# Score products in a row, program order on TensorE in both attentions, and a rotation made by transfers

## The chip, the cores and the metric

One core of a Trainium2 chip runs the whole program. The metric is device time in microseconds (us) of one execution; a measurement gives the median of several. The engines are TensorE (PE; its weight loads are listed apart as PEld), VectorE (DVE), ScalarE (ACT), GpSimd (POOL) and SyncE (SP), which issues the DMAs.

## The reference, cut to what matters

Sequence 512, width 1024, float32, two decoder stacks of two layers each. Two of the four mixers are attentions with pairs of maps:

```
# differential attention: 8 heads, two maps of width 64 each, shared k and v
s = einsum(q, k) * 64**-0.5 ; causal mask ; p = softmax(s)
a = p[map 0] - lam * p[map 1] ;  o = a @ v ;  o = rms_norm(o, g) * (1 - lambda_init) ;  out = o @ w_out
# sparse attention: 16 heads in 4 groups, rotary on the first 16 of 64 dims
q = rmsnorm(q) ; q_rope = partial_rope(q)
s_s = q_rope @ k_sel ; s_w = q_rope @ k_win          # both causal over 512 keys here: all 8 blocks are selected
out = gate_c * o_c + gate_s * softmax(s_s) @ v_sel + gate_w * softmax(s_w) @ v_win
```

`partial_rope` replaces dims (d, d+8), d < 8, by (x1 cos - x2 sin, x2 cos + x1 sin).

## The kernel before, in words

All activations lie transposed, in arenas of 128 x 512 slots: `arena_r` (fp32r, operands of products) and `arena_f` (fp32), and eight PSUM banks. Dense products split both factors into a high and a low part and make three products (L253 to L255, 128 x 512 each). Weights are streamed from HBM in chunks by SP (L92) and split by ACT (L106) and DVE (L107).

Both attentions run through `attend` (L797). Its units are (head, query tile t) in the differential attention and (tile pair T, query tile t, half hh) in the sparse one. In step s it makes the scores of unit s (`score`, L759) and their softmax, combines unit s-1 on DVE, multiplies unit s-3 with V (`value`, L970 and L1564) and calls `finish`, then `each` puts in other work, and last it transposes the maps of unit s-2 (L828) and copies them from PSUM (L832 on DVE, L834 on ACT). The other work are generators in `fill_q`: dense products of the next head's queries or of the output, a few products at each step.

`score` makes for each of the two maps the product with the high part of k, the product with the low part (L772), and a bf16 product of the identity with the causal mask, 128 columns wide (L777). For t below 2 both maps lie in one bank.

After a head's last query tile, `finish` of the differential attention copies the output from PSUM on ACT (L991), squares it on ACT (L993) and sums the columns on TensorE (L289). After heads 3 and 7 a root and a reciprocal follow on ACT and DVE (last L1003), and TensorE spreads the result over the columns (L312). A head's queries leave their dense product through DVE (L903), ACT (L906, twice) and DVE (L907, twice).

In the sparse attention `chain` (L1276) normalises and rotates one 128-row tile, one stage at each step while the tile before it is in `attend`: square, column sums (L1284) with a power on POOL (L1291) and a copy on ACT (L1293), transposes (L1297) and a scaling on DVE (L1299), the permutation as an fp32 product (L1303) with the multiplication by the sines (L1305), then `qout`: the rotated queries and a small attention over compressed keys (L1451, L1475).

In which order an engine works is mostly decided when the program is built: a list scheduler places every instruction as early as its own estimate of times allows, so an instruction of a later step can stand ahead of one that waits. Inside `in_order()` (L370) TensorE keeps the order in which the Python code issues its instructions; the other engines stay free. Before, that is used in `tail` (L326) and `group_halves` (L425) alone, not in `attend`.

Of the kernel before, what the change touches and what calls it, by code (L numbers as in the profile page):

```python
# [211 lines left out]
class Build:  # L212
    def __init__(self, nc, tc, ctx, src, vat):
        self.nc, self.tc, self.src, self.vat = nc, tc, src, vat
        pool = ctx.enter_context(tc.tile_pool(name="sb", bufs=1))
        psum = ctx.enter_context(tc.tile_pool(name="ps", bufs=1, space=bass.MemoryType.PSUM))
        self.pool = pool

        def sb(name, shape, dt=F32):
            return pool.tile(shape, dt, name=name, tag=name)  # L220

        self.sb = sb
        self.fill_q = deque()
        ra = sb("arena_r", [128, N_R, S], F32R)
        fa = sb("arena_f", [128, N_F, S])
        self.R = Arena([ra[:, i] for i in range(N_R)])
        self.F = Arena([fa[:, i] for i in range(N_F)])
        self.fa = fa
        self.P = Arena([psum.tile([128, S], F32, name=f"bank{i}", tag=f"bank{i}") for i in range(8)])
        self.W = Stream(nc, tc, pool, src["w"], src["w"].shape[0])  # L230
        self.vec = sb("vec", list(src["vec"].shape))
        self.cst = sb("cst", list(src["cst"].shape))
        self.small = sb("small", [128, 112])
        self.keep = sb("keep", [128, 16])
        self.sm_n = 0
        self.x = self.F.take(KD)
        self.xd = nc.dram_tensor("x_wait", (KD, 128, S), F32, kind="Internal").ap()
# [218 lines left out]
    def mm(self, out, a, b, start):  # L456
        self.nc.tensor.matmul(out, a, b, start=start, stop=False, skip_group_check=True)  # L457
# [298 lines left out]
        yield  # L756


    def score(self, q2, k2, t):  # L759

        n = 128 * (t + 1)
        banks = self.P.take(1 if t < 2 else 2)
        outs = []
        for c in range(2):
            if t < 2:
                o = banks[0].a[:, c * 256:c * 256 + n]
            else:
                o = banks[c].a[:, :n]
            first = c == 0 or t >= 2
            if isinstance(k2[c], (tuple, list)):  # L770
                for i, k in enumerate(k2[c]):
                    self.nc.tensor.matmul(o, q2[c][:, t * 128:(t + 1) * 128], k[:, :n], start=first and i == 0, stop=False,  # L772
                                          skip_group_check=True)
            else:
                self.nc.tensor.matmul(o, q2[c][:, t * 128:(t + 1) * 128], k2[c][:, :n], start=first, stop=False,
                                      skip_group_check=True)
            self.nc.tensor.matmul(o[:, n - 128:], self.ident_b, self.causal_b, start=False, stop=True,  # L777
                                  skip_group_check=True)
            outs.append(o)
        return banks, outs  # L780

    def softmax(self, banks, outs):
# [14 lines left out]
    def attend(self, units, score, combine, value, finish, fill=1, lag=1, share=True, each=None):  # L797

        nc = self.nc
        st = [None] * len(units)  # L800

        def comb(i):
            if 0 <= i < len(units):
                st[i] = combine(units[i], *st[i])

        for s in range(len(units) + lag + 1):
            if s < len(units):
                banks, outs = score(units[s])
                st[s] = self.softmax(banks, outs)
            comb(s - 1)  # L810
            i = s - lag - 1
            if 0 <= i < len(units):
                value(units[i], st[i])
                finish(units[i])
                st[i] = None
            if each is not None:
                each(s)
            else:
                self.fill(fill)
            i = s - lag  # L820
            if 0 <= i < len(units):
                t = units[i][1]
                n = 128 * (t + 1)
                res = []
                for c, m in enumerate(st[i]):
                    b = self.P.get()
                    for kt in range(t + 1):
                        nc.tensor.transpose(b.a[:, kt * 128:(kt + 1) * 128], m.a[:, kt * 128:(kt + 1) * 128], self.ident)  # L828
                    m.free()
                    d = self.F.get()  # L830
                    if share and (i + c) % 2 == 0:
                        nc.vector.tensor_copy(d.a[:, :n], b.a[:, :n])  # L832
                    else:
                        nc.scalar.activation(d.a[:, :n], b.a[:, :n], AF.Copy)  # L834
                    b.free()
                    res.append(d)
                st[i] = res


    def diff(self, update):  # L840
# [47 lines left out]
        khi, qs = {}, {}  # L888
# [48 lines left out]
        def score(u):  # L937
            h, t = u
            if t == dt[0] and h > 0:
                self.fill_all(qg[h])  # L940
                if h == 4:
                    self.fill_all(vg[3])
                    free([s for p in pk.xs for s in p])
                elif h == 2:
                    self.fill_all(vg[2])
            if t == dt[0] and h < 7:
                self.fill_q.append(qg[h + 1])
                if h < 2:
                    self.fill_q.append(vg[h + 2])
            if t == dt[2] and h < 7:  # L950
                kpack(h + 1)
            return self.score([q.a for q in qs[h]], [[khi[h][c].a, klo[h % 2][c].a] for c in range(2)], t)

        def combine(u, ps, sm):
            n = 128 * (u[1] + 1)
# [269 lines left out]
    def nsa(self, update):  # L1225
# [4 lines left out]
        V = [F.run(2) for _ in range(2)]  # L1230
        va = [self.fa[:, v[0].i:v[0].i + 2].rearrange("p a n -> p (a n)") for v in V]
        vb = [v.rearrange("p (t c) -> p t c", t=4) for v in va]
        kpad = [[R.take(2) for _ in range(4)] for _ in range(2)]
        for c in range(2):
            for g in range(4):
                lo = 64 * (1 - g % 2)
                nc.gpsimd.memset(kpad[c][g][1].a[lo:lo + 64].bitcast(F32), 0.0)
        C, Sn, misc = self.table(6), self.table(7), self.table(8)
        perm, bones = misc.a[:, 0:128], misc.a[:, 128:130]
        w2 = misc.a[:, 256:512]  # L1240
# [32 lines left out]
        nc.vector.tensor_tensor(rs2, rs, rs, op=ALU.mult)  # L1273
        nc.vector.tensor_scalar(rs2, rs2, 1.0 / 64, None, op0=ALU.mult)

        def chain(t, g, scale, out):  # L1276


            sq = F.get()
# [18 lines left out]
            sq.free()  # L1298
            nc.vector.scalar_tensor_tensor(t.a, t.a, self.v(g), b.a, op0=ALU.mult, op1=ALU.mult)  # L1299
            b.free()  # L1300
            yield
            b = P.get()
            nc.tensor.matmul(b.a, perm, t.a, start=True, stop=True)  # L1303
            rot = F.get()
            nc.vector.tensor_tensor(rot.a, b.a, Sn.a, op=ALU.mult)  # L1305
            b.free()
            yield from out(t, rot)
            t.free()
            rot.free()

        def split(src, m, both, hi, lo):

            r, o = slice(64 * m, 64 * m + 64), slice(64 - 64 * m, 128 - 64 * m)
            nc.scalar.activation(hi[r], src[r], AF.Copy)
            if both:
                nc.scalar.activation(hi[o], src[r], AF.Copy)
                nc.vector.tensor_tensor(lo[r], src[r], hi[r], op=ALU.subtract)
            else:
                nc.vector.tensor_tensor(lo[o], src[r], hi[r], op=ALU.subtract)

        def kout(c, i):
            def f(t, rot):
                nc.vector.tensor_tensor(t.a, t.a, C.a, op=ALU.mult)
                nc.vector.tensor_tensor(t.a, t.a, rot.a, op=ALU.add)
                for m in range(2):
                    split(t.a, m, True, kpad[c][2 * i + m][0].a, kpad[c][2 * i + m][1].a)
                yield
            return f

# [78 lines left out]
        raw = {}  # L1408
# [89 lines left out]
        def ahead(T):  # L1498
            while ("q", T) not in raw or side:
                self.fill(1)  # L1500
            ready.append((T, chain(raw.pop(("q", T)), "q_g", 0.125, qout(T))))

        def advance(n=1):
            while n and ready:
# [21 lines left out]
        def score(u):  # L1526
            T, t, hh = u
            g = 2 * (T // 4) + hh
            if (hh, t) == (0, to[0]):
                while ready and ready[0][0] <= T:  # L1530
                    advance()
                qp[T] = R.take(2)
                for m in range(2):
                    split(qr[T].a, m, False, qp[T][m].a, qp[T][m].a)
                qr[T].free()
            return self.score([qp[T][hh].a] * 2, [[s.a for s in kpad[c][g]] for c in range(2)], t)

        def combine(u, ps, sm):
            T, t, hh = u
# [149 lines left out]
def tables():  # L1689
# [14 lines left out]
    for o in (0, 8, 64, 72):  # L1704
        t[6, o:o + 8], t[7, o:o + 8] = np.cos(ang), np.sin(ang)
    for o in (0, 64):
        for d in range(8):
            t[8, o + d + 8, o + d] = -1.0
# [56 lines left out]
```

## Time and profile before

| | us |
|---|---|
| runs | 2692.94, 2693.13, 2695.53 |
| median | 2693.13 |
| the profiled execution | 2693.81 |
| its span, first to last instruction | 2692.0 |

Busy time of each engine in that span: PE 2657.0 us, DVE 1677.4, ACT 1197.9, POOL 117.9. A row of the timeline gives the start, the duration, the engine, the line, the operation with its tiles and shapes, how many are merged, and in brackets the idle time of the engine ahead of it with what ended it. Durations of products overlap, because they are pipelined; what one costs is read from the starts of neighbours. An fp32 product that is neither fp32r nor a transpose shows as two in the trace (L289, L970, L1284, L1303, L1451, L1564): the one permutation product of a chain is "x2". The differential attention lies at 858 to 1036 us, the sparse one at 2082 to 2305 us.

### The profile page before, as it was taken

The numbers are of one execution on the slowest core, as the hardware profiler recorded it, in microseconds if no ns is written. First come the engines' busy times: TensorE is split into PE (matmuls) and PEld (weight loads), VectorE is DVE, ScalarE is ACT, GpSimd is POOL, SyncE is SP. The second block draws the span as 40 slices with busy tenths as digits, with TensorE's granted clock in tenths as the row PEclk, the third lists the DMA queues.
The fourth block names the chain that finished last, engine by engine and source line by source line (L and its number), as shares of the span: only waits on it lengthen the run. The fifth ranks groups of instructions, "written<-read, shape, count | busy, mean of one in ns | idle before, by whom it ended". The sixth has DMA issues, their size and how long they took to land.

```text
span 2692.0 us, 34895 instructions
## 1 busy us (share of the span) xinstructions
PE 2657.0 (99%) x13803; PEld 2203.9 (82%) x13803; DVE 1677.4 (62%) x2765; ACT 1197.9 (44%) x1940; POOL 117.9 (4%) x125
## 2 busy tenths in 40 slices
PE   9999999999999999999999999999999999999999
PEld 8888888888888878788888588888887777888887
DVE  6545557827665677845748966445447788564453
ACT  5443334424445674534433244323347676442331
POOL 0000000000001100000003200000001111000000
PEclk9999999999999999999999999999999999999999
DMA  5222221332222112222223322223343101222222
GB/s 180 80 81 100 85 77 66 110 101 95 97 94 86 56 40 84 89 101 94 98 93 104 108 78 94 94 100 114 119 140 118 40 9 44 75 94 95 101 94 86
DMA packets 73252, 243.41 MB, mean 90 GB/s; under 512 B 9216, under 2 KB 12160, under 8 KB 73088
## 3 DMA queue, kind: packets, MB, share of 16 engines
q1 hardware_dynamic: 73088, 241.18, 26.7%
q8 instruction: 108, 1.77, 0.3%
q14 instruction: 56, 0.46, 0.1%
HBM read 229.63 MB, written 4.19 MB: 87 GB/s over the span
## 4 chain that ended last, share of the span: by engine, by line
PE 89%; DVE 7%; ACT 2%; issue 1%; POOL 0%; DMA 0%; SPq 0%; POOLq 0%; ACTq 0%; DVEq 0%
PE bank L253 24%; PE bank L255 23%; PE bank L254 23%; PE bank L473 3%; PE bank L474 3%; PE bank L477 3%; PE bank L457 2%; PE bank L772 2%; DVE bank L1084 1%; PE bank L1564 1%; PE bank L828 1%; PE bank L1073 1%; PE bank L289 1%; DVE w_spl L107 1%; DVE arena_r L907 1%
## 5 line engine op out<-in xcount | busy, mean ns | idle before, releaser
L253 PE MATMUL bank<-arena_r,w_spl 128*128 128x512 f32 (+1 forms) x2732 | 1060.3, 388 | 4.6 <-ACT w_spl L106 2.6
L254 PE MATMUL bank<-arena_r,w_spl 128*128 128x512 f32 (+1 forms) x2732 | 1053.3, 386 | 0.7 <-DVE arena_r L265 0.7
L255 PE MATMUL bank<-arena_r,w_spl 128*128 128x512 f32 (+1 forms) x2732 | 1050.8, 385 | 0.7 <-DVE w_spl L107 0.7
L106 ACT ACTIVATE w_spl<-w_raw 128x1024 fp32r<-128x1024 f32 (+1 forms) x424 | 448.3, 1057 | 751.1 <-PE bank L254 456.0
L107 DVE TENSOR_TENSOR w_spl<-w_raw,w_spl 128x1024 fp32r<-128x1024 f32 (+1 forms) x414 | 507.1, 1226 | 422.2 <-ACT w_spl L106 419.3
L253 PEld LDWEIGHTS bank<-arena_r,w_spl 128*128 128x128 f32 x2732 | 514.6, 188 | 108.1 <-ACT w_spl L106 4.8
L255 PEld LDWEIGHTS bank<-arena_r,w_spl 128*128 128x128 f32 x2732 | 514.2, 188 | 102.9 <-DVE w_spl L107 1.6
L254 PEld LDWEIGHTS bank<-arena_r,w_spl 128*128 128x128 f32 x2732 | 514.5, 188 | 98.2 <-issue 1.4
L644 DVE SCALAR_TENSOR_TENSOR arena_f<-arena_f,vec 128x510 f32<-128x510 f32 (+1 forms) x264 | 195.2, 748 | 3.4
L264 ACT ACTIVATE arena_r<-arena_f 128x512 fp32r<-128x512 f32 (+1 forms) x153 | 91.9, 610 | 187.7 <-DVE arena_f L672 152.4
L473 PE MATMUL bank<-arena_r,w_spl 128*128 128x512 f32 (+1 forms) x350 | 136.5, 391 | 2.9 <-ACT arena_r L264 1.9
L667 DVE TENSOR_TENSOR arena_f<-bank,arena_f 128x512 f32<-128x512 f32 x88 | 60.8, 691 | 125.9 <-PE bank L255 125.9
L474 PE MATMUL bank<-arena_r,w_spl 128*128 128x512 f32 (+1 forms) x350 | 136.2, 390 | 0.0
L265 DVE TENSOR_TENSOR arena_r<-arena_f,arena_r 128x512 fp32r<-128x512 f32 (+1 forms) x153 | 100.8, 672 | 35.1 <-ACT arena_r L264 34.5
L792 ACT ACTIVATE arena_f<-bank,small 128x128 f32<-128x128 f32 (+3 forms) x192 | 99.5, 525 | 48.4 <-DVE small L789 42.8
L253 PE MATMUL bank<-w_spl,arena_r 128*128 128x256 f32 (+2 forms) x352 | 116.2, 331 | 2.1 <-ACT arena_r L1351 1.5
L669 ACT ACTIVATE arena_f<-arena_f 128x512 f32<-128x512 f32 x88 | 55.5, 631 | 138.8 <-DVE arena_f L644 138.8
L642 ACT ACTIVATE arena_f<-arena_f,vec 128x512 f32<-128x512 f32 x132 | 106.1, 810 | 19.6 <-DVE arena_f L663 17.6
L255 PE MATMUL bank<-w_spl,arena_r 128*128 128x256 f32 (+2 forms) x352 | 114.1, 326 | 0.1
L254 PE MATMUL bank<-w_spl,arena_r 128*128 128x256 f32 (+2 forms) x352 | 113.9, 324 | 0.0
L663 DVE TENSOR_TENSOR arena_f<-bank,arena_f 128x512 f32<-128x512 f32 x88 | 60.7, 689 | 81.3 <-PE bank L255 72.8
L772 PE MATMUL bank<-arena_r 128*128 128x128 f32 (+3 forms) x384 | 96.5, 356 | 2.4 <-DVE arena_r L907 2.3
(229 smaller groups left out, 2806.2 us busy)
## 6 DMA issues: line engine op xcount, KB each, us to landing
w_raw<-w SPq DMA_DIRECT2D x422, 512.0 KB, 3.5
arena_f<-tab SPq DMA_DIRECT2D x10, 256.0 KB, 3.5
arena_f<-x SPq DMA_DIRECT2D x8, 256.0 KB, 6.3
x_wait<-arena_f SPq DMA_DIRECT2D x8, 256.0 KB, 2.2
arena_f<-x_wait SPq DMA_DIRECT2D x8, 256.0 KB, 2.6
out<-arena_f SPq DMA_DIRECT2D x8, 256.0 KB, 2.0
arena_r<-arena_f SPq DMA_DIRECT2D x20, 64.0 KB, 2.0
arena_r<-arena_f SPq DMA_DIRECT2D x20, 63.9 KB, 2.0
```

The source lines that it names most:

```text
L106: self.nc.scalar.activation(hi, r, AF.Copy)
L107: (self.lo_engine or self.nc.vector).tensor_tensor(lo, r, hi, op=ALU.subtract)
L253: mm(out, a[0], b[0], start=start, stop=False, skip_group_check=skip)
L254: mm(out, a[0], b[1], start=False, stop=False, skip_group_check=skip)
L255: mm(out, a[1], b[0], start=False, stop=stop, skip_group_check=skip)
L265: self.nc.vector.tensor_tensor(l, src, h, op=ALU.subtract)
L473: mm(b, w[0], hi[:, sl], start=(k == 0 and sl.start == 0), stop=False, skip_group_check=True)
L474: mm(b, w[1], hi[:, sl], start=False, stop=False, skip_group_check=True)
L642: nc.scalar.activation(c.a, u.a, AF.Identity, bias=self.v(cb, j), scale=self.v(cw, 2 * nj + j))
L644: nc.vector.scalar_tensor_tensor(c.a[:, d:], u.a[:, :S - d], self.v(cw, (2 - d) * nj + j), c.a[:, d:], op0=ALU.mult, op1=ALU.add)
L772: self.nc.tensor.matmul(o, q2[c][:, t * 128:(t + 1) * 128], k[:, :n], start=first and i == 0, stop=False, skip_group_check=True)
L792: nc.scalar.activation(p.a[:, :n], outs[c], AF.Exp, bias=mx[:, c:c + 1], accum_out=sm[:, c:c + 1])
```

## The change

Three edits. (1) `score` issues the products of both maps first and then the masks; for t below 2 there is one mask product of 256 columns for both maps, and in the sparse attention, where both maps have the same queries, also one product per part of k for both maps, twice as wide. (2) The loop of `attend` stands in `in_order()`; the transposes have become a function `turn`, called at the same place. (3) In `chain`, for query tiles 1 to 7, the permutation product is replaced by a POOL memset and four transfers of 8 rows from SBUF to SBUF, issued by SP one stage earlier; the sign moves into the table of sines. The keys of the sparse attention are allocated as neighbours so that (1) can read both maps in one access.

```
     def score(self, qs, ks, t):
...
+        outs = [banks[0].a[:, c * n:(c + 1) * n] if one else banks[c].a[:, :n] for c in range(2)]
+        if one and len(qs) == 1:
+            o = banks[0].a[:, :2 * n].rearrange("p (c n) -> p c n", c=2)
+            for i, k in enumerate(ks):
+                mm(o, qs[0][:, sl], self.ra[:, k[0].i:k[0].i + 2, :n], start=(i == 0), stop=False, skip_group_check=True)
+        else:
+            for c in range(2):
+                for i, k in enumerate(ks):
+                    mm(outs[c], qs[c % len(qs)][:, sl], k[c].a[:, :n], start=(i == 0 and (c == 0 or not one)), stop=False,
+                       skip_group_check=True)
+        if one:
+            o = banks[0].a[:, :2 * n].rearrange("p (c n) -> p c n", c=2)[:, :, n - 128:]
+            mm(o, self.ident_b, self.causal_b.unsqueeze(1).to_broadcast([128, 2, 128]), start=False, stop=True,
+               skip_group_check=True)
+        else:
+            for o in outs:
+                mm(o[:, n - 128:], self.ident_b, self.causal_b, start=False, stop=True, skip_group_check=True)
...
-        for s in range(len(units) + lag + 1):
+        with self.in_order():
+            for s in range(len(units) + lag + 1):
...
-            yield
-            b = P.get()
-            nc.tensor.matmul(b.a, perm, t.a, start=True, stop=True)
-            rot = F.get()
-            nc.vector.tensor_tensor(rot.a, b.a, Sn.a, op=ALU.mult)
...
+            if copy:
+                rot = F.get()
+                nc.gpsimd.memset(rot.a, 0.0)
+                for o in (0, 64):
+                    for d in (0, 8):
+                        nc.sync.dma_start(rot.a[o + d:o + d + 8], t.a[o + 8 - d:o + 16 - d])
+                yield
+                nc.vector.tensor_tensor(rot.a, rot.a, Sn.a, op=ALU.mult)
+                yield from out(t, rot)
+                rot.free()
...
-            ready.append((T, chain(raw.pop(("q", T)), "q_g", 0.125, qout(T))))
+            ready.append((T, chain(raw.pop(("q", T)), "q_g", 0.125, qout(T), T > 0)))
```

## Rows read from the trace of the kernel before

**Rows 1.** The page: TensorE's busy time, and the chain that ended last, by engine
```profile
PE 2657.0 (99%) x13803; PEld 2203.9 (82%) x13803; DVE 1677.4 (62%) x2765; ACT 1197.9 (44%) x1940; POOL 117.9 (4%) x125
...
PE 89%; DVE 7%; ACT 2%; issue 1%; POOL 0%; DMA 0%; SPq 0%; POOLq 0%; ACTq 0%; DVEq 0%
```

**Rows 2.** Windows, both attentions: length, then busy time (instructions) by engine
```profile
857.90:1036.30 178.40, 172.00 (x1105) 146.51 (x1104) 132.43 (x294) 117.91 (x259) 17.68 (x12) 1.00 0.16 55
2081.90:2305.00 223.10, 220.29 (x1737) 172.66 (x1737) 181.40 (x518) 154.30 (x449) 28.70 (x36) 1.00 0.09 30
```

**Rows 3.** Timeline of PE, sparse attention: score products of t = 1, 0, 3
```profile
2211.34 0.48 PE L772 MATMUL bank<-arena_r 128*128 128x256 f32 x2
...
2211.71 0.48 PE L772 MATMUL bank<-arena_r 128*128 128x256 f32 x2
...
2213.41 0.42 PE L772 MATMUL bank<-arena_r 128*128 128x128 f32 x2
...
2213.71 0.42 PE L772 MATMUL bank<-arena_r 128*128 128x128 f32 x2
...
2222.55 0.71 PE L772 MATMUL bank<-arena_r 128*128 128x512 f32 x2
...
2223.14 0.71 PE L772 MATMUL bank<-arena_r 128*128 128x512 f32 x2
```

**Rows 4.** The chain in order of time: dense 512-column products back to back
```profile
27.49 0.91 PE bank L477 x4
```

**Rows 5.** Timeline of PE: a permutation product and what follows it
```profile
2232.12 1.02 PE L1303 MATMUL bank<-arena_f 128*128 128x512 f32 x2
2232.97 1.00 PE L1451 MATMUL bank<-arena_f 128*128 128x64 f32 x8
```

**Rows 6.** The page, DMA issues: the transfers in SBUF nearest to the new ones
```profile
arena_f<-arena_f SPq DMA_DIRECT2D x8, 128.0 KB, 3.1
```

**Rows 7.** The same transfers by source line: ns that SP takes to issue one
```profile
L1267 SPq DMA_DIRECT2D arena_f<-arena_f x8: 517/568/595, 1997.5 to 2007.3; - x8
```

**Rows 8.** Groups of POOL: the memset of one slot
```profile
L1375 POOL MEMSET arena_f<- 128x512 f32 x1 | 0.5, 534 | 35.3 <-DVE arena_f L280 35.3
```

**Rows 9.** Timeline of PE in `group_halves`, which keeps program order already
```profile
414.19 3.82 PE L457 MATMUL bank<-arena_r,w_spl 128*128 128x256 f32 x18 [1.45 <-ACT arena_r L267]
```

**Rows 10.** Timelines of PE and ACT behind the last value product of heads 1 and 0
```profile
910.49 0.36 PE L253 MATMUL bank<-w_spl,arena_r 128*128 128x256 f32 x1
...
911.26 0.59 ACT L993 ACTIVATE arena_f<-bank 128x512 f32<-128x512 f32 x1
...
887.84 0.48 PE L254 MATMUL bank<-arena_r,w_spl 128*128 128x512 f32 x1
...
889.79 0.60 ACT L993 ACTIVATE arena_f<-bank 128x512 f32<-128x512 f32 x1
```

**Rows 11.** Timeline of PE: behind the queries' products, and the first scores (heads 0, 3)
```profile
857.85 0.39 PE L253 MATMUL bank<-arena_r,w_spl 128*128 128x512 f32 x1
...
860.92 0.44 PE L772 MATMUL bank<-arena_r 128*128 128x128 f32 x2
...
920.16 0.61 PE L970 MATMUL bank<-arena_f 128*128 128x128 f32 x4
...
924.00 0.44 PE L772 MATMUL bank<-arena_r 128*128 128x128 f32 x2 [0.58 <-DVE arena_r L907]
```

**Rows 12.** Timelines of PE and DVE behind the column sums of head 7
```profile
1006.32 0.48 PE L254 MATMUL bank<-arena_r,w_spl 128*128 128x512 f32 x1
...
1007.96 0.17 DVE L1003 TENSOR_SCALAR small<-small 128x16 f32<-128x16 f32 x1
```

**Rows 13.** Timeline of PE: a chain's transposes, and the work standing ahead of them
```profile
2228.56 0.79 PE L254 MATMUL bank<-arena_r,w_spl 128*128 128x512 f32 x1
...
2230.33 0.65 PE L1297 MATMUL bank<-cst,arena_f 128*128 128x128 f32 x4
```

**Rows 14.** Windows, right behind the wait of rows 9 (PEclk is the third number from the end)
```profile
413.90:417.40 3.50, 3.21 (x15) 3.21 (x16) 3.23 (x7) 1.99 (x4) 0.00 (x0) 0.51 0.02 6
```

More of the change, by code (lines that the diff above doesn't have):

```diff
@@ L227, in __init__ @@
         self.F = Arena([fa[:, i] for i in range(N_F)])
-        self.fa = fa
+        self.fa, self.ra = fa, ra
         self.P = Arena([psum.tile([128, S], F32, name=f"bank{i}", tag=f"bank{i}") for i in range(8)])
@@ L756, in rows_gen, with score @@
         yield
-    def score(self, q2, k2, t):
+    def score(self, qs, ks, t):
+        mm = self.nc.tensor.matmul
         n = 128 * (t + 1)
[L762 to L779, printed above, removed]
+        sl = slice(t * 128, (t + 1) * 128)
+        one = t < 2
+        banks = self.P.take(1 if one else 2)
+        outs = [banks[0].a[:, c * n:(c + 1) * n] if one else banks[c].a[:, :n] for c in range(2)]
[15 more added lines that the diff above has]
+                mm(o[:, n - 128:], self.ident_b, self.causal_b, start=False, stop=True, skip_group_check=True)
         return banks, outs
@@ L804, in comb @@
                 st[i] = combine(units[i], *st[i])
-        for s in range(len(units) + lag + 1):
[L807 to L837, printed above, removed]
@@ new lines, in turn @@
+        def turn(i):
+            t = units[i][1]
+            n = 128 * (t + 1)
+            res = []
+            for c, m in enumerate(st[i]):
+                b = self.P.get()
+                for kt in range(t + 1):
+                    nc.tensor.transpose(b.a[:, kt * 128:(kt + 1) * 128], m.a[:, kt * 128:(kt + 1) * 128], self.ident)
+                m.free()
+                d = self.F.get()
+                if share and (i + c) % 2 == 0:
+                    nc.vector.tensor_copy(d.a[:, :n], b.a[:, :n])
+                else:
+                    nc.scalar.activation(d.a[:, :n], b.a[:, :n], AF.Copy)
+                b.free()
+                res.append(d)
+            st[i] = res
@@ new lines, in attend @@
+        with self.in_order():
+            for s in range(len(units) + lag + 1):
+                if s < len(units):
+                    banks, outs = score(units[s])
+                    st[s] = self.softmax(banks, outs)
+                comb(s - 1)
+                i = s - lag - 1
+                if 0 <= i < len(units):
+                    value(units[i], st[i])
+                    finish(units[i])
+                    st[i] = None
+                if each is not None:
+                    each(s)
+                else:
+                    self.fill(fill)
+                i = s - lag
+                if 0 <= i < len(units):
+                    turn(i)
@@ L951, in score @@
                 kpack(h + 1)
-            return self.score([q.a for q in qs[h]], [[khi[h][c].a, klo[h % 2][c].a] for c in range(2)], t)
+            return self.score([q.a for q in qs[h]], [khi[h], klo[h % 2]], t)
         def combine(u, ps, sm):
@@ L1232, in nsa @@
         vb = [v.rearrange("p (t c) -> p t c", t=4) for v in va]
-        kpad = [[R.take(2) for _ in range(4)] for _ in range(2)]
+        kpad = [[R.run(2) for _ in range(2)] for _ in range(4)]
         for c in range(2):
@@ L1236, in nsa @@
                 lo = 64 * (1 - g % 2)
-                nc.gpsimd.memset(kpad[c][g][1].a[lo:lo + 64].bitcast(F32), 0.0)
+                nc.gpsimd.memset(kpad[g][1][c].a[lo:lo + 64].bitcast(F32), 0.0)
         C, Sn, misc = self.table(6), self.table(7), self.table(8)
@@ L1274, in nsa, with chain @@
         nc.vector.tensor_scalar(rs2, rs2, 1.0 / 64, None, op0=ALU.mult)
-        def chain(t, g, scale, out):
+        def chain(t, g, scale, out, copy=False):
             sq = F.get()
@@ L1300, in chain @@
             b.free()
-            yield
-            b = P.get()
-            nc.tensor.matmul(b.a, perm, t.a, start=True, stop=True)
-            rot = F.get()
-            nc.vector.tensor_tensor(rot.a, b.a, Sn.a, op=ALU.mult)
-            b.free()
-            yield from out(t, rot)
+            if copy:
[8 more added lines that the diff above has]
+                rot.free()
+            else:
+                yield
+                b = P.get()
+                nc.tensor.matmul(b.a, perm, t.a, start=True, stop=True)
+                rot = F.get()
+                nc.vector.tensor_tensor(rot.a, b.a, Sn.a, op=ALU.mult)
+                b.free()
+                yield from out(t, rot)
+                rot.free()
             t.free()
-            rot.free()
         def split(src, m, both, hi, lo):
@@ L1325, in f @@
                 for m in range(2):
-                    split(t.a, m, True, kpad[c][2 * i + m][0].a, kpad[c][2 * i + m][1].a)
+                    split(t.a, m, True, kpad[2 * i + m][0][c].a, kpad[2 * i + m][1][c].a)
                 yield
@@ L1535, in score @@
                 qr[T].free()
-            return self.score([qp[T][hh].a] * 2, [[s.a for s in kpad[c][g]] for c in range(2)], t)
+            return self.score([qp[T][hh].a], kpad[g], t)
         def combine(u, ps, sm):
@@ L1706, in tables @@
     for o in (0, 64):
+        t[7, o:o + 8] *= -1.0
         for d in range(8):
-            t[8, o + d + 8, o + d] = -1.0
+            t[8, o + d + 8, o + d] = 1.0
             t[8, o + d, o + d + 8] = 1.0
```

## The prediction

> **What bounds it now.** I read the page first: TensorE is busy for 99% of the span, and 89% of the chain that ended last is its own work [rows 1]. So a product taken away is worth what it takes on TensorE, and time in which TensorE waits is added one for one; work on ACT, DVE or POOL counts only where TensorE waits for it. Next the windows of the two attentions, where all edits lie: TensorE idles 178.4 - 172.0 = 6.4 us in the first and 223.1 - 220.3 = 2.8 us in the second [rows 2]. These 9.2 us are most of what a better order could win. Then I laid TensorE's timeline beside the order in which the code issues, to see where the two differ. They differ much in the first attention and little in the second, and wherever an instruction runs late, the work that fills its place came from a later step.
>
> **Edit 1, score products.** From one map's first product to the next map's takes 0.30 us at 128 columns, 0.37 at 256 and 0.59 at 512 [rows 3]. A 512-column product in an unbroken row takes 0.91 / 4 = 0.23 us [rows 4], so a mask between products costs 0.59 - 0.46 = 0.13. A 256-column product then takes (0.37 - 0.13) / 2 = 0.12, a 128-column one 0.085. A mask of 256 columns isn't in the trace; it lies between 0.13 and 0.13 plus half a 256-column product, and I take 0.19, the upper end, because it streams twice the columns.
> - Sparse, t = 0, 16 units: before 0.60, after 2 x 0.12 + 0.19 = 0.43: 2.7 us.
> - Sparse, t = 1, 16 units: before 0.74, after 2 x 0.23 + 0.19 = 0.65: 1.4 us.
> - Differential, t below 2, 16 units: 0.60 becomes 4 x 0.085 + 0.19 = 0.53 and 0.74 becomes 0.67: 1.1 us.
> - t = 2 and 3, 48 units: the same six products; only the second mask no longer breaks a row. That is worth between nothing and 0.13; I take 0.05, nearer to nothing since it still streams 128 columns: 2.4 us.
>
> Together **-7.6 us**, bounds -4 and -11; a loss is excluded, since no unit gets more products or columns. The first map's softmax starts some 0.5 us later; the lag of two steps covers it, and without that cover it would cost 0.5 us a unit.
>
> **Edit 3, rotation.** From a permutation product to the next one 2232.97 - 2232.12 = 0.85 us [rows 5], seven times: **-6.0 us**. In its place come seven memsets of 0.53 us [rows 8], on POOL, which is busy for 4% of the span [rows 1], and 28 transfers on SP. Nearest to them are transfers of 128 KB, with 0.57 us to issue [rows 7] and 3.1 us to landing [rows 6]. The last of four is then in place 4 x 0.57 + 3.1 = 5.4 us behind the scaling, and the multiplication by the sines stands one stage behind it, 2232.12 - 2230.33 = 1.8 us in the shortest case [rows 5, 13]. DVE keeps its queue in order: at worst it stands 3.6 us for each chain, and the reductions and scalings of the units queued behind it stand too. The chain runs a whole tile ahead and the transposes two steps behind, which hides that; I take nothing, and 7 x 1.4 = 10 us as the other end, where two steps hide 2.2 us of each. SP's weight loads behind these transfers come 2.3 us later, with chunks loaded ahead. Where no dense work is left TensorE may not gain all of the 0.85, so the end on the gain's side is -6 and none beyond.
>
> **Edit 2, program order.** Where it is in force already, TensorE does stand still with other work at hand: 1.45 us in front of L457 [rows 9]. So I go through the places where the free order has filled a gap, and charge what the gap would be.
> - First scores: TensorE is done with the queries' product at 857.85 and the packed queries come at 860.92 [rows 11]. 3.1 us.
> - Column sums of `finish`: in program order they stand right behind the last value product, while ACT must first copy and square the output. For head 1 that is 911.26 + 0.59 - 910.49 = 1.36 us, for head 0, where ACT has softmaxes in between, 889.79 + 0.60 - 887.84 = 2.55 us [rows 10]. Eight heads: 10.9 to 20.4; I take **10.9**, the case with ACT free, because ACT is planned anew.
> - Scores of later heads: from the queries' last product to their first use 924.00 - 920.16 = 3.8 us [rows 11]. Program order puts nothing of weight between for head 3 and some 1.6 us for head 2 (twelve products of 256 columns at 0.12 and a transposition). For head 4 it is one score group (2 x 0.59) and a transposition, 1.5, and for heads 5 to 7 two dense steps (6 x 0.23) more, 2.9. Waits: 3.8 + 2.2 + 2.3 + 3 x 0.9 = **11.0**; head 1's queries are done long before.
> - Spreading: at head 7 the root and reciprocal take 1007.96 + 0.17 - 1006.32 = 1.8 us behind the sums [rows 12]. At head 3 DVE has queries to pack meanwhile, so I take twice that there. 5.4 us.
>
> That is 30.4 us in the first attention. Today's idle time there, 6.4 us, goes, since it is part of the same waits: **+24.0**. In the second attention the order is nearly the program's already; what differs each time is a chain's transposes, 2230.33 - 2228.56 = 1.8 us late behind the power on POOL and a copy on ACT [rows 13]. Six chains: 0 to 10.6 us, and I take 1.2 each, because a waiting TensorE lets the others catch up: 7.2 less 2.8 idle today, **+4.4**.
>
> The clock makes waits dearer. [...] I charge two such stretches, **+3.4**, for the two longest waits (3.1 and 3.8 us).
>
> **Sum.** -7.6 - 6.0 + 24.0 + 4.4 + 3.4 = +18.2. The profiled execution took 2693.81 us (span 2692.0), 0.7 over the median; so 2712.0. The wait for the sums of `finish` is late next: nothing can be filled in there any more.
>
> **Rivals.**
> - *The waits shrink (0.16, 2684 us).* The other engines are planned round TensorE's new order, so what it waits for is placed first. ACT is busy for 118 of 178 us [rows 2], so there is room. With a third of the 37.6 us of waits, 12.5, less 9.2 of idle today, no clock loss and 13.6 gained, 2683.5. It decides at waits of 22.8 in all, and it is faster by the bound below 17.4. Against it: the 1.36 us of rows 10 is already copy and square back to back.
> - *The order does not bind (0.06, 2680 us).* If the guard is only a preference, edits 1 and 3 remain: 2693.8 - 13.6. Rows 9 speak against it.
> - *Every longer wait costs the clock (0.14, 2730 us).* If nine more of the some 20 waits drop the clock as in rows 14, 9 x 1.7 = 15.3 is added; with the transfers' other end on top 2740, with a part of it 2732. This trace shows waits followed by the lower level, and most of the new ones are about as long as that of rows 9 or longer. [...]
> - *Even (0.14).* Waits of 17 to 28 us: 2688.4 to 2699.2.
>
> **Numbers.** 0.2% is 5.4 us, about what a measurement of this kernel can tell from no change. The forecast, 2700 to 2725, has the remaining 0.50. Faster 0.16 + 0.06 = 0.22, same 0.14, slower 0.50 + 0.14 = 0.64. The range goes from 2684, which leaves out the lower half of the first rival and the second, to 2732, beyond which half of the third lies; within the forecast's case alone it is 2700 to 2725.
>
> **What would show it.** Right: L289 gets idle time of about 1.4 us at each head, ended by ACT L993; L772 with 128 columns waits for DVE L907 at heads 0 and 2 to 7; L312 waits for L1003. Idle time in the first attention's window rises from 6 to about 30 us, and the window grows by some 20. Two maps of the sparse t = 0 stand 0.43 us instead of 0.60 before the next work. L1303 falls from 24 to 10, with no idle time of DVE at L1305 of over 1 us. Wrong: if idle time in that window stays under 15 us, the waits were mis-sized; if TensorE's instructions still leave the code's order, the guard does not bind; if the window of the sparse attention grows by over 10 us, the transfers or the chains' waits were.

## The result, and the profile after

| | before | after |
|---|---|---|
| median, us | 2693.61 (4 runs) | 2757.17 (2753.34 to 2759.55, 4 runs) |
| the profiled execution, its span | 2693.81, 2692.0 | 2753.34, 2751.6 |

After takes 1.0234 of the time of before, 95% interval 1.0221 to 1.0246. The forecast was 2712 us, in a range of 2684 to 2732: the sign was right, the size was not. The page of the changed kernel, busy time and the chain that ended last [rows 1]:

```profile
PE 2663.9 (97%) x13677; PEld 2210.0 (80%) x13677; DVE 1678.6 (61%) x2765; ACT 1198.9 (44%) x1940; POOL 126.7 (5%) x132
...
PE 85%; DVE 9%; ACT 3%; issue 1%; POOL 1%; SPq 0%; DMA 0%; POOLq 0%; ACTq 0%; DVEq 0%
```

TensorE makes 126 instructions fewer and yet is busy 7 us longer, in a span 60 us longer. The windows of both attentions, between the same pieces of work as in [rows 2]; columns are length, busy time by engine, then the granted clock third from the end:

```profile
857.90:1093.40 235.50, 194.58 (x1090) 164.91 (x1090) 134.72 (x294) 118.02 (x259) 19.52 (x12) 0.90 0.12 41
2139.00:2364.60 225.60, 206.76 (x1627) 163.36 (x1625) 180.66 (x517) 153.87 (x448) 35.24 (x42) 0.99 0.10 31
```

Nearly all of it lies in the differential attention: 235.5 - 178.4 = +57.1 us, of which 40.9 - 6.4 = 34.5 are waiting of TensorE and 194.6 - 172.0 = 22.6 are products that take longer, at a mean clock of 0.90 instead of 1.00. The sparse one grew by 2.5: 13.5 us less work, 16.0 more waiting. The waits of the first, in the groups of that window that have idle time (last field: idle ahead, and what ended it):

```profile
L775 PE MATMUL bank<-arena_r 128*128 128x128 f32 (+3 forms) x128 | 31.8, 366 | 11.5 <-DVE arena_r L915 11.5
L978 PE MATMUL bank<-arena_f 128*128 128x128 f32 x160 | 27.2, 303 | 14.7 <-DVE arena_f L821 10.5 <-ACT arena_f L823 3.7
...
L289 PE MATMUL bank<-vec,arena_f 128*128 128x1 f32 x66 | 9.5, 264 | 13.0 <-ACT arena_f L1001 13.0
L312 PE MATMUL bank<-cst,small 128*128 128x128 f32 x32 | 5.6, 349 | 1.7 <-DVE small L1011 1.7
```

The scores (L775) and the column sums (L289) wait about as forecast. L978 is `value` (L970 before), whose wait the forecast did not have at all. One of its two longest, 4.20 us (the other, 4.46 us at 991.06, also stands behind L915), in the timelines of DVE, then of PE:

```profile
872.46 1.22 DVE L107 TENSOR_TENSOR w_spl<-w_raw,w_spl 128x1024 fp32r<-128x1024 f32 x1
873.71 3.31 DVE L915 TENSOR_TENSOR arena_r<-arena_f,arena_r 64x512 fp32r<-64x512 f32 x2
876.94 0.28 DVE L821 COPY arena_f<-bank 128x128 f32<-128x128 f32 x1
```

```profile
871.84 0.27 PE L817 MATMUL bank<-cst,arena_f 128*128 128x128 f32 x1
871.87 1.17 PE L775 MATMUL bank<-arena_r 128*128 128x512 f32 x4
872.88 0.28 PE L783 MATMUL bank<-causal_b,ident_b 128*128 128x128 bf16 x2
877.37 0.76 PE L978 MATMUL bank<-arena_f 128*128 128x128 f32 x2 [4.20 <-DVE arena_f L821]
```

The transposition is done near 872.1; its copy takes 0.28 us, but stands in DVE's queue behind a split of weights and the packing of the next queries (L915, 3.31 us). In program order only one unit's scores lie between a transposition and the `value` that uses it, so TensorE stands 4.2 us. The copy starts at 876.94 and not at 872.1, behind work that DVE began at 872.46 and 873.71. Whether the copies would come in time if DVE took them ahead of the packing was not tried.

### The profile page after: what moved, and what is told of

It reads as the page before. It is cut to its first block, busy times and chain, and to the rows that moved or that the text cites. A ratio compares the mean times of both kernels' runs of the same rounds, so it can differ in the third digit from the quotient of the medians.

```text
span 2751.6 us, 34727 instructions
## 1 busy us (share of the span) xinstructions
PE 2663.9 (97%) x13677; PEld 2210.0 (80%) x13677; DVE 1678.6 (61%) x2765; ACT 1198.9 (44%) x1940; POOL 126.7 (5%) x132
## 4 chain that ended last, share of the span: by engine, by line
PE 85%; DVE 9%; ACT 3%; issue 1%; POOL 1%; SPq 0%; DMA 0%; POOLq 0%; ACTq 0%; DVEq 0%
PE bank L253 23%; PE bank L255 23%; PE bank L254 23%; PE bank L473 3%; PE bank L474 3%; PE bank L477 3%; DVE bank L1092 2%; PE bank L457 2%; ACT arena_f L796 1%; PE bank L289 1%; DVE small L793 1%; PE bank L775 1%; DVE w_spl L107 1%; DVE arena_f L1566 1%; PE bank L817 1%
## 5 line engine op out<-in xcount | busy, mean ns | idle before, releaser
L793 DVE TENSOR_REDUCE small<-bank 128x1 f32<-128x128 f32 (+3 forms) x192 | 85.2, 482 | 27.6 <-PE bank L783 14.2
```

Source lines behind the costliest of these rows:

```text
L793: nc.vector.tensor_reduce(mx[:, c:c + 1], outs[c], op=ALU.max, axis=AX.X, negate=True)
```

## The experiments

All times of before in these comparisons are medians of 2694.1 to 2694.5 us. "Stage" is the time from the first score product to the last `value` product of an attention.

**1 to 4: which part costs.** The loop's guard `with self.in_order():` is taken away (e1), kept in one attention only (e2, e3), or put alone into the kernel before (e4).

```
-        with self.in_order():
+        with self.in_order() if order else nullcontext():
```

> The changed kernel without program order in `attend`: the score products and the rotation alone. Theory (the loss is program order, in the differential attention, and the two other edits gain what they were priced at): 2693.6 - 13.6 = 2680 us, differential attention within 3 us of 178.4, no stretch at half the clock in it. Rival (the transfers hold DVE or the joint masks delay the softmaxes): 2690 to 2700, with idle time of TensorE in the sparse attention well above 2.8 us.

> The changed kernel with program order in the differential attention only. Theory: the differential attention keeps its 235.5 us and the sparse one comes down to some 210 (223.1 less the gains there of 4.1 to 6 of the scores and 6 of the rotation); 2680 + 57 + 2 = 2739 us. Rival (the loss lies in the sparse attention too, its growth of 2.5 us being a loss of 16 that eats the two gains): the same place, so the split between this run and the next decides: this one then gains some 16 on the changed kernel's 2757, that is 2741. Rival (order is harmless alone and it is the joint mask that makes the scores late): 2757.

> The changed kernel with program order in the sparse attention only. Theory: 2680 + 16 = 2696 us (the sparse attention keeps its 225.6 us, of which 14 us is what the two edits gained and program order took again); the differential attention as in the kernel before. If the two edits gain little and order costs little there, 2692 as well but with the free-order run near 2690.

> The kernel before with program order in both attentions and nothing else. Theory: the parts add up, so 2757 + 13.6 = 2771 us. Rival (the joint masks and the later first map cause the waits in program order): clearly under 2757.

Measured: 2691.11 (ratio 0.9988, 0.9979 to 0.9997), 2754.0, 2697.33 and 2767.66 us. Program order in the differential attention costs 2754.0 - 2691.1 = 63 us, in the sparse one 6. The theory stands for the loss. Its other half fell: without program order the two other edits gain 3 us and not 13.6, and mainly for that e2 came 15 us above its 2739. With program order they gain 2767.7 - 2757.2 = 10.5. Windows of e1, both stages; then of after, the first stage:

```profile
860.46:1001.79 141.33, 134.58 (x886) 115.43 (x886) 110.52 (x257) 99.44 (x231) 17.13 (x12) 1.00 0.16 49
2080.02:2301.68 221.66, 214.49 (x1629) 163.61 (x1627) 181.61 (x518) 153.83 (x449) 35.79 (x42) 1.00 0.11 32
```

```profile
860.70:1060.29 199.59, 161.47 (x897) 135.86 (x898) 113.02 (x257) 100.45 (x231) 19.52 (x12) 0.88 0.10 35
```

Nearly the same instructions take 134.6 us in the free order at full clock and 161.5 in program order at 0.88, 26.9 us more. That this is nearly all the clock, the next runs show.

**5 and 12: what the clock costs.** In the differential attention TensorE makes unread products where it would wait. In e5 those for heads 1 to 3 stood one head ahead of the waits they were meant for; e12 mended that and halved the rest.

```
+        def warm(n):
+            if n:
+                b = P.get()
+                for _ in range(n):
+                    nc.tensor.matmul(b.a, pq.xs[0][0].a[:, :128], pq.xs[1][0].a, start=True, stop=True)
+                b.free()
...
+            warm(ahead_v.get((h, t), 0))
...
+            warm(ahead_c[h])
             self.colsum(stat["b"], [sq], 4 * (h % 4), h % 4 == 0)
```

> The changed kernel, and at the places in the differential attention where TensorE waits longest (nine units' `value`, the column sums of all heads, the first scores of six heads) it first makes products that nobody reads, 174 of 512 columns at 0.23 us, about as long as each wait; the waited-for work stays where it is. Theory (the clock falls behind these waits, and the some 40 us at the lower level cost about half of that): the stretches at half the clock in the differential attention go, TensorE's idle time there falls from 41 to some 10 us, its products take about as much in its place, and the time falls to 2757 - 20 = 2737 us, between 2730 and 2745. Rival (the low clock only fills time that TensorE would have waited anyway, because DVE and ACT set the pace): 2752 to 2765.

> As the first run with unread products, with 73 of them in place of 174: about half at each place, and for the first scores at heads 0, 2, 3 and 4, where the trace of the changed kernel has the waits. There 22.5 us of the lower clock's cost went from TensorE's products, but 40.3 us of unread ones came in for 26.5 us of waiting, so the time fell by 8 only; open is whether the other 14 us were the unread products' own overshoot or would have been waited anyway. Theory (the lower clock lies on the path): the clock stays up at most places and the time falls below that run's 2749 us, to 2735 to 2742. Rival (at the full clock TensorE only comes earlier to the same waits, and the clock's own part is some 9 us): 2746 to 2752, with idle time and unread products together still near 55 us.

Measured: 2749.23 and 2753.50 us. Windows of the stage, and behind each the unread products alone in it (length, busy time on PE, then on PEld), e5, then e12:

```profile
862.11:1052.96 190.85, 176.55 (x1036) 146.31 (x1037) 113.73 (x257) 100.28 (x231) 19.29 (x12) 0.98 0.11 37
...
862.11:1052.96 190.85, 37.20 (x140) 25.17 (x141) 0.98 0.11 37
```

```profile
859.69:1052.63 192.94, 167.55 (x963) 139.09 (x964) 113.05 (x257) 100.17 (x231) 19.63 (x12) 0.94 0.11 36
...
859.69:1052.63 192.94, 19.70 (x67) 11.76 (x68) 0.94 0.11 36
```

By the starts of neighbours the unread products take 36.5 us of the stage in e5 and 19.8 in e12; with those ahead of its first score product and behind its last `value` it is 40.3 and 21.5. Are they longer than the waits that they fill? The longest group of e5, and the one at the same place in e12, in the timelines of PE:

```profile
982.54 4.34 PE L979 MATMUL bank<-arena_r 128*128 128x512 f32 x18
988.03 0.49 PE L992 MATMUL bank<-arena_f 128*128 128x128 f32 x2 [1.15 <-DVE arena_f L821]
```

```profile
982.13 2.30 PE L979 MATMUL bank<-arena_r 128*128 128x512 f32 x9
986.89 0.76 PE L992 MATMUL bank<-arena_f 128*128 128x128 f32 x2 [2.46 <-DVE arena_f L821]
```

TensorE idles behind them before the copy comes. So it does behind nearly every group of e12 and half of those of e5; set against the semaphores in the trace, about 2 of the 36.5 us in e5 ran past what was waited for, and none in e12.

| stage, us | own work | waits + unread products | sum |
|---|---|---|---|
| after, clock 0.88 | 161.5 | 38.1 | 199.6 |
| e12, clock 0.94 | 147.7 | 25.4 + 19.8 = 45.2 | 192.9 |
| e5, clock 0.98 | 140.1 | 14.3 + 36.5 = 50.8 | 190.9 |

The clock did fall because of the waits: where they are filled the stage has 0.98 (e5) and 0.94 (e12), and 0.88 in after. In program order the same work takes 161.5 us at 0.88 and 140.1 at 0.98. But of these 21 us that the clock gives back, 12.7 come back as waiting, at most 2 of them the unread products' own: TensorE only reaches the same late copies and sums earlier. Net the clock is worth 6.7 us of the stage in e12 and 8.7 in e5, or about 11 without the 2 us. At that clock the waits are thus some 49 us, and not the 38 of after.

Of the run's median it is 4 and 8 us, and the 4 of e12 are not clear of the noise (ratios of 1.0206 to 1.0237, against 1.0221 to 1.0246 for after). The three profiled executions differ by 2.4 us at most, in part because the sparse attention, with nothing changed in it, took 226.2 us in after and 229.2 and 230.2 in e12 and e5. e5 fell between both theories, e12 a little above the rival's range: the rival's reason is the nearer one, though of its some 55 us of waits and unread products together e12 shows 45.

**6, 7, 8, 11: which wait.** Program order stays; one distance each is made longer in the differential attention: `value` and `finish` behind the dense products (e6), `finish` alone behind them (e7), the next queries' product finished a step earlier (e8), `value` behind the dense products and `finish` a step later still (e11).

```
+                each(s)
                 if 0 <= i < len(units):
                     value(units[i], st[i])
                     finish(units[i])
                     st[i] = None
-                each(s)
...
+                if 0 < i <= len(units):
+                    finish(units[i - 1])
+                each(s)
+                if 0 <= i < len(units):
+                    value(units[i], st[i])
+                    st[i] = None
...
+            if t == dt[3] and h < 7:
+                self.fill_all(qg[h + 1])
```

> The changed kernel with one thing of the program order altered in the differential attention: `value` and `finish` stand behind `each` (the dense products) of the same step, not ahead of it, so that the copies out of PSUM have some 2 us more; the slots of a head's queries and keys come free right behind its last scores. Theory (the waits of `value` for copies that stand in DVE's queue behind the packing of queries are a term of their own, 14.7 us, with some 10 us of half clock behind them): L978's idle time under 4 us, the time 2757 - 11 - 4 = 2742 us. Rival (DVE is behind by as much anyway, and the wait goes to the column sums or the next scores): idle time in the stage still 38 us or more, 2755.

> The changed kernel with the column sums of `finish` behind `each` of the same step in the differential attention (`value` stays ahead of it), slots freed as in the run above. Theory (the column sums' 14.3 us of waits, and the five of ten half-clock stretches that stand behind them): L289's idle time under 4 us, 2757 - 11 - 9 = 2737 us. Rival (a wait taken away there is only met again at the next one): 2750 or more.

> The changed kernel with the next head's queries finished ahead of the scores of t = 3 of the head before, one step earlier. Theory (the scores' waits for packed queries, 12.2 us, of which the first head's 2.9 stay, and the half clock behind three of them): L775's idle time 4 to 6 us, 2757 - 7 - 4 = 2746 us. Rival (the packing then stands in front of the same copies and softmaxes on DVE, and `value` waits longer): 2755 or more, L978's idle time above 18 us.

> The changed kernel, with program order kept and respaced in the differential attention: `value` behind `each`, and the column sums of `finish` one step later, behind the next scores and ahead of `each`'s dense products. Theory (each wait is a distance in program order that is too short, and the clock falls only behind such waits): below the 2731.7 us of the run with `value` late alone by most of the 14.7 us that L289 still waits there and some of the 40 us at half clock, so 2712 us, between 2705 and 2720, with L289's idle time under 6 us. Rival (the sums wait as long at their new place): 2728 or more.

Measured: 2731.72 (e6), 2749.29 (e7), 2760.74 (e8), 2718.88 us (e11). The stage's window of e6 and its groups with idle time; then the stage's window of e11, and two of its groups:

```profile
860.22:1036.15 175.93, 154.21 (x897) 133.54 (x898) 108.46 (x257) 100.27 (x231) 16.87 (x12) 0.88 0.13 40
...
L775 PE MATMUL bank<-arena_r 128*128 128x128 f32 (+3 forms) x128 | 33.9, 390 | 8.0 <-DVE arena_r L915 7.9
L981 PE MATMUL bank<-arena_f 128*128 128x128 f32 x160 | 24.7, 287 | 0.1
L289 PE MATMUL bank<-vec,arena_f 128*128 128x1 f32 x56 | 8.1, 266 | 14.7 <-ACT arena_f L1003 14.7
```

```profile
860.30:1022.89 162.59, 146.25 (x896) 126.81 (x896) 112.07 (x257) 100.39 (x231) 18.44 (x12) 0.93 0.13 43
```

```profile
L986 PE MATMUL bank<-arena_f 128*128 128x128 f32 x160 | 23.7, 279 | 0.2
L289 PE MATMUL bank<-vec,arena_f 128*128 128x1 f32 x56 | 7.4, 253 | 6.5 <-ACT arena_f L1008 6.5
```

In e6 `value`'s wait is gone and 25.5 us with it, more than the 14.7 it showed: in the stage of 175.9 us, 16.4 of waiting and 7.3 of work. The sums still wait 14.7; e11 moves them too, and the time falls by another 13, into its range, though they still wait 6.5, a little over the 6 of its theory. e7 missed its 2737 and stands just under its rival's 2750: the sums' wait only fell to 7.5, the spreading waits 2 us more and the scores 1. `value` waits 10.2 us there in place of 14.7, without having been moved; why was not looked into. e8 went its rival's way in time, with 16.3 us at `value` and not the 18 that it named: the scores of head 2 no longer wait, but a `value` behind them does (1.2 us); at head 3 no dense work was left behind the earlier product, so it ended one short step of 1.7 us ahead, and the scores still wait 3.2.

**9 and 10: where the two edits' gain goes in the free order.** e9 is e1 with all rotations by the permutation product, e10 is e1 with the old `score`.

> The new `score` alone: no program order, all rotations by the permutation product. The two edits without program order gained 3.3 us, though TensorE's score and permutation products took 14.9 us less. Theory A (what is freed is given back by the free order, whichever edit frees it: more idle time and more changes between kinds of products): about 2 us faster than before, 2692, with the score products 9 us shorter. Theory B (the score edit gains its 9 us and the transfers cost what they free and more): 2685 to 2687.

> The rotation by transfers alone: `score` issues its products in the old order (product, product, mask for each map), no program order. Theory A: 1 us faster than before, 2693 us. Theory B (the transfers, or the memset and the issue behind them, make the chain late, so the transposes at its end and the queries wait): 2697 to 2700, with idle time at the chain's transposes and at the transposes of the small attention of over 3 us more than before.

Measured: 2691.39 (ratio 0.9989, 0.9980 to 0.9999) and 2692.76 us (0.9996, 0.9987 to 1.0005). Theory A in both: each frees what it was priced at and gains little. By the starts of neighbours, score and mask products fall from 90.1 to 81.9 us over the run in e9; in e1's sparse stage they and the permutations fall by 12.8, and the stage by 1.7. Waits rise there by 4.4, and the other products get dearer by 6.4. Half of that is `value`:

| `value` in the sparse stage | us by the starts of neighbours | rows broken by other work |
|---|---|---|
| before | 46.1 | 41 |
| e1, free order | 49.3 | 55 |
| e3, program order | 46.1 | 33 |
| e15, program order respaced | 42.2 | 32 |

The last `value` product of a row takes 203 ns to the next work, one inside a row 63 to 65 on average (in before and e1), so 14 more breaks are 1.9 of the 3.2 us. Breaks are not all of it: e3 has about as few as e15 and takes 3.9 us more, and that difference is not explained. That the broken rows come from the list scheduler's own estimate of times was not tried.

**13 to 16: program order with its distances stretched, sparse attention alone.** e13 moves `value` and `finish` behind `each`; e14 also gives the chain one step more ahead of its transposes and the small attention one ahead of its own; e15 also splits the next queries two steps early and returns the chain's bank; e16 is e15 with all rotations by the permutation product.

```
+                if order:
+                    each(s)
                 if 0 <= i < len(units):
                     value(units[i], st[i])
...
+            if copy:
+                b.free()
+                yield
+                b = P.get()
             for i in range(4):
                 nc.tensor.transpose(b.a[:, i * 128:(i + 1) * 128], sq.a[:, i * 128:(i + 1) * 128], self.ident)
...
             advance()
+            if s % 8 == 6 and T < 7:
+                qsplit(T + 1)
```

> Program order in the sparse attention alone, with `value` and `finish` behind `each` there; free order in the differential attention. Program order there left TensorE 207 us of work in place of the 214.5 of the free order, and 18.8 us of waiting in place of 7.2. Theory (the waits of `value` are again a distance that is too short): L1583's 4.6 us go, so 2697 - 4 = 2693 us. Rival (the chain's waits grow by as much): 2697.

> The same, and each chain gets one more step between the power and copy and its transposes, with the small attention's softmax in one stage and one step more ahead of its transposes. Theory: L1305's 9.9 and L1494's 3.7 us of waiting mostly go too, the rows of products stay unbroken, and the two edits' gain is kept: 2683 us, between 2680 and 2688, faster than both kernels. Rival (DVE sets the pace of this stage once TensorE doesn't wait): 2690 or more, with new waits at the scores or at `value`.

> The run before last's pattern with two more distances put right: the rotated queries of the next tile are split into their parts two steps ahead of their first scores, and a chain gives back its bank of PSUM between its column sums and its transposes. In that run the scores waited 8.2 us, for the split and for banks, and 10 us stood at half the clock. Theory (program order with every distance long enough keeps the two edits' gain): 2689.6 - 5 - 3 = 2682 us, between 2678 and 2686. Rival (DVE's or ACT's pace sets this stage, the wait moves on): 2688 or more.

> The same with all rotations by the permutation product. Theory (in an order without waits the rotation by transfers gains what it was priced at): 6 us more than the run with transfers. Rival (the chain is early enough either way and TensorE's time is given back): within 2 us of it.

Measured: 2705.96, 2689.63, 2684.43 (ratio 0.9964, 0.9951 to 0.9976) and 2693.26 us (0.9997, 0.9987 to 1.0007). Waits of the chain's transposes in e13; waits of the scores in e14; the sparse stage's window in e15, and in e16:

```profile
L1305 PE MATMUL bank<-cst,arena_f 128*128 128x128 f32 x28 | 6.0, 350 | 18.5 <-ACT arena_f L1301 18.5
```

```profile
L775 PE MATMUL bank<-arena_r 128*128 128x384 f32 (+1 forms) x128 | 37.1, 409 | 7.3 <-DVE arena_r L1340 4.6 <-ACT arena_f L796 2.7
```

```profile
2079.20:2295.33 216.13, 206.33 (x1639) 161.20 (x1639) 182.59 (x517) 154.02 (x449) 35.08 (x43) 0.99 0.11 33
```

```profile
2078.91:2302.39 223.48, 211.23 (x1647) 162.90 (x1647) 181.37 (x517) 154.78 (x449) 29.98 (x37) 0.99 0.09 29
```

e13 went the wrong way: `value` waits 2.0 us in place of 4.6, but the chain's transposes 18.5 in place of the 9.9 of e3, and the clock is 0.94 in that stage. e14 stretches that distance and, as its rival had it, meets the scores, 1.6 us above its theory's range; e15 stretches those and lands in its range. It is the fastest version here, 10.0 us under before. Between e16 and e15 the rotation by transfers gains 8.8 us, more than its 6.0 of products.

## Why the prediction was wrong in size

- **Edit 1, -7.6:** right as TensorE's time: 8.2 us less by e9. For the sparse t = 0 the two maps stand 0.53 us ahead of the next work, and not 0.43. But the 0.60 taken for before left out the break to work of another kind: ahead of `value` it was 2214.13 - 2213.41 = 0.72, so the gain there, 0.19, is the forecast 0.17. In the timelines of before and of after:

```profile
2213.41 0.42 PE L772 MATMUL bank<-arena_r 128*128 128x128 f32 x2
...
2214.13 0.33 PE L1564 MATMUL bank<-arena_f 128*64 128x128 f32 x2
```

```profile
2161.67 0.48 PE L771 MATMUL bank<-arena_r 128*128 128x256 f32 x2
2161.99 0.28 PE L779 MATMUL bank<-causal_b,ident_b 128*128 128x256 bf16 x1
2162.20 1.56 PE L1583 MATMUL bank<-arena_f 128*64 128x128 f32 x16
```

- **Edit 3, -6.0:** right as TensorE's time: the permutation products fall by 5.9 us, and DVE does not stand at the multiplication by the sines (no idle time ahead of L1316 in seven). SP takes 0.62 us for each of the 28 issues, against 0.57 taken from [rows 7]. Ahead of the seven groups SP stands 68.6 us for the scalings, 22.9 at most, where the forecast had the weight loads only 2.3 us later; in the sparse attention TensorE waits for no weights.
- **The step "a product taken away is worth what it takes on TensorE"** does not hold in the free order: there the 13.6 us were worth 3 (e1). With program order they were worth 10.5 (after against e4).
- **Edit 2, first scores and scores of later heads, 14.1:** right in the main, 11.5 measured, at heads 0, 2 to 4, 6 and 7.
- **Edit 2, column sums, 10.9:** low, 13.0 in the window. The case with ACT free was taken, and it isn't: at head 0 two softmaxes stand between the copy and the square.

```profile
897.79 0.60 ACT L999 ACTIVATE arena_f<-bank 128x512 f32<-128x512 f32 x1 [1.31 <-PE bank L978]
898.29 0.57 ACT L796 ACTIVATE arena_f<-bank,small 128x384 f32<-128x384 f32 x1
...
898.85 0.58 ACT L796 ACTIVATE arena_f<-bank,small 128x384 f32<-128x384 f32 x1
...
899.40 0.60 ACT L1001 ACTIVATE arena_f<-bank 128x512 f32<-128x512 f32 x1
```

- **Edit 2, spreading, 5.4:** high, 1.7.
- **The step that failed** is the list itself, "I go through the places where the free order has filled a gap". It was made from rows in which something late was seen, and `value` is hardly late in the kernel before (1.7 us of idle time ahead of L970), since the free order puts dense products ahead of it. In program order it stands one unit's scores behind its copies, which queue behind the packing of queries: 14.7 us of visible waits, none forecast, and 25.5 us once moved (e6). The waits came to 40.9 us in place of 30.4, and by e5 to some 49 in the stage at a clock of 0.98.
- **The clock, +3.4:** no run shows this term by itself: it is two times 1.7 us, an estimate from [rows 14], 3.5 x (1 - 0.51). In its place the stage of after has 199.6 us at a mean clock of 0.88. As work it was mis-sized, and so was the rival's 15.3 on top of it, nine times the same estimate: 21 to 27 us (after against e5 and e1). The clock's own worth is 7 to 11 us of the stage (e5, e12), between the two. The slow products hid waits that the list had missed. The stage's clock is 0.88 in after against 1.00 in e1, but the clock did not fall behind every long wait, as the last section shows. The same estimate for this stage, its length times the share of the clock that is lost, is (1 - 0.88) x 199.6 = 24 us; as TensorE's work that agrees, as time it does not.
- **Sparse attention, +4.4:** right in sum by luck: e3 against e1 gives 6.2. Waits there rise from 7.2 to 18.9 us, 9.9 of them at the chain's transposes and the rest mostly at `value` and the small attention, while the products take 5.6 less, which no term had. With both edits' gains, 5.7 and 6.0, the window was to fall by 7.3 against before; it grew by 2.5, as those gains shorten it by 1.7 only in the free order.
- **The rivals:** that the order does not bind fell with e1. Its 2680 us was wrong as well: the free order gives the gains back. In the third, 2712 + 15.3 + 10 is 2737 and not 2740.

## What to carry to other kernels

When an order is frozen, list for every instruction of the frozen engine what it waits for, how far ahead that is issued and what queues in front of it on the other engine; places that show no wait today are those that the free order covers. Judge a kind of wait by moving it, not by its idle time: taken away, it can be worth more (25.5 for 14.7) or uncover the next (e13). And price a cut in one engine's work against the order it runs in: the rotation was worth 2 us or nothing in the free order, and 8.8 in a frozen order with long enough distances.

## What was not expected of the hardware

A wait's length does not tell here whether the clock falls behind it. In after, behind 2.36 us at 900.06 the next products keep 1.00, while behind another 2.36 us, at 1029.13, they start at 0.50; and behind only 1.82 us at 954.93 the clock goes to 0.50 some 2.3 us later. Windows behind the three; then dense products at 0.50 (behind the first scores' wait, 2.89 us) and at 1.00 (behind that of 2.36 us at 900.06):

```profile
901.00:904.40 3.40, 3.40 (x18) 2.63 (x19) 0.29 (x1) 0.52 (x1) 0.32 (x1) 1.00 0.00 0
1029.13:1032.53 3.40, 3.40 (x12) 3.11 (x13) 0.35 (x1) 0.00 (x0) 0.00 (x0) 0.50 0.02 5
957.20:960.60 3.40, 3.40 (x13) 2.23 (x11) 2.94 (x4) 2.31 (x3) 1.70 (x1) 0.50 0.00 0
```

```profile
863.25 0.63 PE L253 MATMUL bank<-arena_r,w_spl 128*128 128x512 f32 x1
863.67 0.63 PE L254 MATMUL bank<-arena_r,w_spl 128*128 128x512 f32 x1
...
901.29 0.39 PE L254 MATMUL bank<-arena_r,w_spl 128*128 128x512 f32 x1
901.52 0.39 PE L255 MATMUL bank<-arena_r,w_spl 128*128 128x512 f32 x1
```

At 0.50 a 512-column product stands 0.42 us ahead of the next, at 1.00 it is 0.23. What else decides it was not tried.
